# First norm of a two-layer diffusion step: order of the scale's loads, and unsplit weights for the first shift

## Chip, cores and metric

The kernel runs on one core of a Trainium2 chip. The metric is device time in microseconds, the median of several runs of one program. TensorE (PE) multiplies, VectorE (DVE), ScalarE (ACT) and GpSimd (POOL) do the elementwise work, and SyncE (SP) issues nearly all transfers, in order.

## The reference, cut to what matters

The model is one inference step of two hybrid layers over 128 context tokens and 512 latent tokens, 1024 wide. Each layer begins so:

```python
mod = silu(cond) @ w_ada[l] + b_ada[l]          # cond: c_ctx for context tokens, c for latent tokens
shift1, scale1, gate1, shift2, scale2, gate2 = split(mod, 6)
h = rmsnorm(x, norm1_g) * (1.0 + scale1) + shift1
xbc, dv, ... = split(h @ w_in, ...)             # one input projection
```

The rest (latent attention, differential attention, a scan, the output projection, a squared-ReLU network) is the same before and after the change. All of it is in float32.

## The kernel before

**Layout.** Features lie on the 128 partitions and the 640 tokens on the free axis, so x is eight tiles (k = 0 to 7) of 128 x 640, called `x`. Weights come in halves of 128 x 512: `wr` is a raw half, `wh` its rounded high part and `wl` the remainder. A product of float32 accuracy is made of three fast matmuls, `wh`*`zh`, `wh`*`zl` and `wl`*`zh`, where `zh` and `zl` are the same two parts of the scaled input. PE runs each of them in two column halves of 320, so one k of one unit takes six matmuls, and one k of two units twelve (`fm`, L312, matmul at L318).

**Scale and shift of the first norm.** `AdaPE` (L355) computes one 1024-wide slice of `mod` for both conditions: `first` is the scale (slice 1), `second` the shift (slice 0). The slice comes in two halves of 512 columns, and a half needs eight pieces `war` of 128 x 512 (256 KB), one per k. A step splits a piece into `wah` (ACT, L377) and `wal` (DVE or POOL, L378) and multiplies both by the small `sch` and `scz` (PE, L379 and L380, tile `adap`, four output rows, 512 columns). After eight steps `half` (L385) copies the result (`adarow`, ACT), turns it by four transposes (`adat`, PE), copies and sums (`adah`), and `ada_finish` (L335) adds the bias (`mod`); for the scale it also makes `amul`, for the shift the parts `shh` and `shl`.

**First products.** x is scaled by `amul` before its mean square is known (`scaled`, L488: `zh` on ACT, `zl` on DVE), and squares (`nsq`) are summed beside it. `first_units` (L546) multiplies `xbc0` and `xbc1` by it. Then `rows` (tile `nss`) and `spread` (tile `nrb`) make the row factors `nR`, and `out` applies them to the product (`un`, DVE). The shift enters the first two units as a product of raw weights and shift (`bshp`, L677), added later. For `xbc2` and `xbc3` the shift is put into the input itself (`normed`, L637: `nt` on DVE, `hhi` on ACT, `hlo` on DVE), so these products need the shift of their own k: k = 0 to 3 its first half, k = 4 to 7 its second. After them come the units `dv` (tile `tm`, L758 to L760).

**What sets the order.** Each engine works through its own queue in order. A scheduler orders the queues by its own estimate of times; `after` asks it to place instructions behind a given one. `LATE` gives how many steps of the shift follow each k of the first products (0, 0, 0, 0, 2, 4, 5, 5), and the rest follow them. `AP1` and `AP0` list the steps whose `wal` POOL makes. SP's queue holds, in this order: the first eight pieces of the scale, the four halves of `xbc0` and `xbc1`, four x tiles, `rows`, eight pieces of the scale, four x tiles, masks, seven raw halves, 16 pieces of the shift. Of the seven raw halves, two are of `xbc2` and five are asked for under the name `xbc3`, of which two are used; the other three are fetched and read by nothing.

Of the kernel before, what the change touches and what calls it, by code (L numbers as in the profile page):

```python
# [21 lines left out]
P = 128  # L22
D = 1024
KD = D // P
# [38 lines left out]
UNIT = {}  # L63
# [41 lines left out]
def build(nc, tc, a, ctx):  # L105
# [63 lines left out]
    def f(ap):  # L169
        return ap.bitcast(F32)  # L170
# [141 lines left out]
    def fm(outs, hi, lo, xh, xl, ks, first, last):  # L312

        for i, k in enumerate(ks):
            wh, wl = hi[:, i * P:(i + 1) * P], lo[:, i * P:(i + 1) * P]
            for w, xx, s, e in ((wh, xh, k == first, False), (wh, xl, False, False), (wl, xh, False, k == last)):
                for o, ts in outs:
                    pe.matmul(o, w, xx[k][:, ts], start=s, stop=e)  # L318

    def fm_unit(hi, lo, xh, xl, cut=None):  # L320
        ps = PA("fm")
# [10 lines left out]
    shh = [cp.tile([P, 2, KD, 2], F32R, name=f"shh{l}") for l in range(DEPTH)]  # L332
    shl = [cp.tile([P, 2, KD, 2], F32R, name=f"shl{l}") for l in range(DEPTH)]

    def ada_finish(l, j, ps, ms=slice(0, KD)):  # L335
# [8 lines left out]
        if j in (0, 3):  # L344
            evac_split(shh[l][:, j // 3, ms], shl[l][:, j // 3, ms], mods[l][:, j, ms])


# [5 lines left out]
    vec.tensor_tensor(out=sch[:, :, 2:4], in0=sc, in1=f(sch[:, :, 0:2]), op=ALU.subtract)  # L353

    class AdaPE:  # L355


        def __init__(self, l, j, on_pool):
# [9 lines left out]
        def step(self, n=1):  # L368
            for _ in range(n):
                if self.n == 2 * KD:  # L370
                    return
                h, k = divmod(self.n, KD)
                if k == 0:
                    self.ps = PB("adap")
                raw = self.raws[self.n]
                hi, lo = Y([P, 512], F32R, name="wah"), Y([P, 512], F32R, name="wal")
                act.copy(out=hi, in_=raw)  # L377
                (pool if self.n in self.on_pool else vec).tensor_tensor(out=lo, in0=raw, in1=f(hi), op=ALU.subtract)  # L378
                pe.matmul(self.ps[:4], sch[:, k, :], hi, start=(k == 0), stop=False)  # L379
                pe.matmul(self.ps[:4], scz[:, k, :], lo, start=False, stop=(k == KD - 1))  # L380
                self.n += 1
                if k == KD - 1:
                    self.half(h)

        def half(self, h):  # L385
            pt = PB("adat")
            row = X([4, 512], name="adarow")
            act.copy(out=row, in_=self.ps[:4])
            for m in range(4):
                pe.transpose(pt[:, 4 * m:4 * m + 4], row[:, m * P:(m + 1) * P], ident[:4, :4])  # L390
            p4 = pt[:, :16].rearrange("p (m q v) -> p m q v", q=2, v=2)
# [150 lines left out]
    def zhalves(ps, c=0):  # L542

        return [(ps[:, 0, c:HT + 2], slice(c, HT + 2)), (ps[:, 1, :HT], slice(HT + 2, T + 2))]

    def first_units(W, names, nrm, then=None, late=None):  # L546

        ps = [PA("fm") for _ in names]
        for k in range(KD):
            with after(nrm.last):  # L550
                if k == 4:
                    nrm.rows()
                if k == 5:
                    nrm.spread()
            if k == 6 and then:
                then()
            for n, p_ in zip(names, ps):
                hi, lo = W(n)
                fm(zhalves(p_, 0 if nrm.early else 2), hi[:, k * P:], lo[:, k * P:], nrm.zh, nrm.zl, [k], 0, KD - 1)
            if late:  # L560
                with after(nrm.mid):
                    late.step(LATE[k])
        return ps

# [6 lines left out]
    def mixing(l, nrm, fill, late=None, raws={}):  # L571
# [82 lines left out]
        W.ahead = AHEAD  # L654
        if late:
            with after(nrm.last):
                late.step(16)
                W.half(4)
            for k in range(3):
                normed(k)  # L660
        else:
            xps = [padded(None, z) for z in zs]
        ps = [PA("fm") for _ in range(2)]
        for k in range(KD):
            mark(f"{l}norm1")
            if k >= 3:
                normed(k)
            mark(f"{l}xbc")
            for j in range(2):
                hi, lo = W(f"xbc{2 + j}")  # L670
                fm(halves(ps[j]), hi[:, k * P:], lo[:, k * P:], hh, hl, [k], 0, KD - 1)
        if late:
            pb_ = PB("bshp")
            for j in range(2):
# [1018 lines left out]
    N_TAIL = 30  # L1693
    AHEAD = 1
    FETCHED, AHEADS = 7, 2
    AP1, AP0 = (1, 4), ()
    FILL = (2, 20, 9), (8, .01, 9)
    ROWS_POOL = ()
    CONV_POOL = ()
    ON_POOL = {f"xbc{j}" for j in range(2, 6)} | {"dv0", "dv1"}  # L1700
    LATE = (0, 0, 0, 0, 2, 4, 5, 5)
    N_STACK = 52
    N_SSD = 34
    N_PROJ = 28
# [260 lines left out]
    for h in range(2):  # L1965
        first.fetch()
        for n_ in ("xbc0", "xbc1") if h == 0 else ():
            for i in range(2):
                raws0[n_].append(G([P, 512], name="wr0"))
                o = UNIT[n_][0] + i * 512  # L1970
                nc.sync.dma_start(raws0[n_][i], a["W"][0, :, o:o + 512])
        for k in range(4 * h, 4 * h + 4):
            load_x(a["xT"], k)
        if h == 0:
            rows0 = load_rows(0)
# [4 lines left out]
    raws0.update({"xbc2": [raw_weights(0, "xbc2", h) for h in range(2)], "xbc3": [raw_weights(0, "xbc3", h) for h in range(NWR - 2)]})  # L1980
    second.fetch()
    second.fetch()
    nrm = Norm(False)
    act.copy(out=identr, in_=id_)
    first.step(8)
    for k in range(4):
        nrm.scaled(0, 0, k)
        if k == 1:
            last = nrm.last
    with after(last):  # L1990
        for k in range(4):
            first.step(2)
            nrm.square(k, vec)
    for k in range(4, 8):
        nrm.scaled(0, 0, k)
        nrm.square(k, vec)
        if k == 4:
            nrm.mid = nrm.last
# [131 lines left out]
```

## Time and profile before

| | us |
|---|---|
| median of 3 runs | 1838.31 (1832.51 to 1839.88) |
| the profiled execution | 1843.01 |
| its span | 1841.2 |
| PE busy | 1752.6 (95%) |
| DVE busy | 1330.3 (72%) |
| ACT busy | 828.8 (45%) |
| POOL busy | 464.5 (25%) |

The span runs from the first to the last instruction of the profiled execution; 1.8 us of its time lie outside. A row of a timeline is one or more like instructions in a row on one engine: start, duration, engine, line, what is written and read, and how many. What stands in brackets is the engine's idle time ahead of it and what ended that. Matmuls are pipelined: the distance between starts is what one costs, and its duration is longer. Matmuls in full float32 are recorded twice. PEclk is the granted clock of TensorE as a share of 2.4 GHz: 1.00 is 2.4 GHz and 0.50 is 1.2 GHz.

### The profile page before, as it was taken

The page shows a single profiled execution, that of the slowest core. Times are in us where ns is not written, and L with a number is a line of the kernel's source. Part 1 is how long each engine was busy: PE and PEld are TensorE (multiplying, and loading weights), DVE is VectorE, ACT ScalarE, POOL GpSimd, SP SyncE. Part 2 cuts the span into 40 slices and gives each one's busy share as a digit, 9 for nine tenths or more (in the row PEclk, how much of TensorE's full clock was granted, in tenths as well). Part 3 has the DMA queues.
Part 4 walks back from the last instruction along what each step waited for, and adds up shares of the span by engine and source line. Part 5 has one row for each costly group of instructions (what it writes and reads, how often), then busy time and mean ns, then how long its engine had stood idle before and what let it go on. Part 6 is the DMA issues. An engine that isn't in the chain of part 4 may idle for free. (4 is left out here: it accounts for less than half of the span.)

```text
span 1841.2 us, 31851 instructions
## 1 busy us (share of the span) xinstructions
PE 1752.6 (95%) x11764; PEld 1659.3 (90%) x11764; DVE 1330.3 (72%) x2788; ACT 828.8 (45%) x1737; POOL 464.5 (25%) x538
## 2 busy tenths in 40 slices
PE   6999999999989999999997999889999999999999
PEld 4798778998989999999997987779999999999998
DVE  6774867568578988685776778989677877475562
ACT  7553327554445452432544443387534445243340
POOL 1433433101120231404135244431003032130400
PEclk8899866899999999999999999889999999999999
DMA  9122113344143437264441232202424242525341
GB/s 336 56 78 71 52 35 88 103 136 146 32 136 117 138 100 260 93 213 154 149 159 48 76 107 68 69 25 84 138 88 127 86 131 81 186 87 161 112 157 56
DMA packets 122732, 209.02 MB, mean 114 GB/s; under 512 B 13392, under 2 KB 32720, under 8 KB 122576
## 3 DMA queue, kind: packets, MB, share of 16 engines
q1 hardware_dynamic: 122016, 206.80, 35.2%
q8 instruction: 93, 1.52, 0.3%
q14 instruction: 63, 0.52, 0.1%
q10 hardware_dynamic: 560, 0.18, 0.0%
HBM read 179.51 MB, written 27.43 MB: 112 GB/s over the span
## 5 line engine op out<-in xcount | busy, mean ns | idle before, releaser
L1775 ACT CAST wh<-wr 128x512 fp32r<-128x512 f32 x232 | 143.9, 621 | 316.0 <-PE fm L1805 205.2
L1805 PE MATMUL fm<-ul,wh 128*128 128x320 f32 x1024 | 235.0, 311 | 10.2 <-DVE ul L307 10.2
L1776 DVE TENSOR_TENSOR wl<-wr,wh 128x512 fp32r<-128x512 f32 x232 | 179.0, 780 | 79.8 <-issue 44.6
L1805 PE MATMUL fm<-uh,wh 128*128 128x320 f32 x1024 | 234.8, 310 | 0.1
L1805 PE MATMUL fm<-uh,wl 128*128 128x320 f32 x1024 | 234.5, 310 | 0.0
L1762 POOL TENSOR_TENSOR wS<-wr,wr 128x512 f32<-128x512 f32 x48 | 78.7, 1639 | 495.2 <-DMA wr<-in_W 213.9
L1805 PEld LDWEIGHTS fm<-ul,wh 128*128 128x128 f32 x1024 | 172.3, 189 | 11.3 <-DVE ul L307 11.3
L427 DVE SCALAR_TENSOR_TENSOR junk<-wa,crow 128x512 f32<-128x512 f32 x256 | 176.7, 739 | 7.4 <-DMA wa<-in_w_adaT 5.7
L1805 PEld LDWEIGHTS fm<-uh,wh 128*128 128x128 f32 x1024 | 172.4, 189 | 0.5 <-issue 0.3
L1805 PEld LDWEIGHTS fm<-uh,wl 128*128 128x128 f32 x1024 | 172.3, 189 | 0.0
L539 DVE SCALAR_TENSOR_TENSOR x<-fm,mod,x 128x128 f32<-128x128 f32 (+2 forms) x192 | 72.5, 432 | 107.7 <-PE fm L1805 104.7
L759 PE MATMUL tm<-wl,hhi 128*128 128x256 f32 (+2 forms) x400 | 120.0, 300 | 5.7 <-POOL wl L297 4.0
L1775 ACT CAST wh<-wS 128x512 fp32r<-128x512 f32 x96 | 59.8, 622 | 141.7 <-PE fm L1805 70.5
L758 PE MATMUL tm<-wh,hhi 128*128 128x256 f32 (+2 forms) x400 | 120.0, 300 | 3.0 <-DVE zth L779 2.4
L760 PE MATMUL tm<-wh,hlo 128*128 128x256 f32 (+2 forms) x400 | 119.2, 298 | 0.0
L296 ACT CAST wh<-wr 128x512 fp32r<-128x512 f32 (+2 forms) x108 | 66.8, 625 | 75.6 <-PE fm L318 34.6
L1805 PE MATMUL ffx<-eh,wh 128*128 128x320 f32 x288 | 89.4, 311 | 0.0
L1805 PE MATMUL ffx<-eh,wl 128*128 128x320 f32 x288 | 88.9, 309 | 0.0
L1805 PE MATMUL ffx<-el,wh 128*128 128x320 f32 x288 | 88.9, 309 | 0.0
L759 PEld LDWEIGHTS tm<-wl,hhi 128*128 128x128 f32 x400 | 80.2, 200 | 8.0 <-POOL wl L297 4.2
L539 DVE SCALAR_TENSOR_TENSOR x<-wo,mod,x 128x128 f32<-128x128 f32 (+1 forms) x144 | 57.0, 432 | 39.0 <-PE wo L318 38.5
L758 PEld LDWEIGHTS tm<-wh,hhi 128*128 128x128 f32 x400 | 80.1, 200 | 5.1 <-DVE zth L779 2.8
(386 smaller groups left out, 4837.1 us busy)
## 6 DMA issues: line engine op xcount, KB each, us to landing
wr<-in_W SPq DMA_DIRECT2D x351, 256.0 KB, 2.8
wa<-in_w_adaT SPq DMA_DIRECT2D x128, 256.0 KB, 4.5
xsave<-x SPq DMA_DIRECT2D x72, 320.0 KB, 2.2
x<-xsave SPq DMA_DIRECT2D x72, 320.0 KB, 4.0
war<-in_w_ada SPq DMA_DIRECT2D x32, 256.0 KB, 5.3
wa<-in_w_ada SPq DMA_DIRECT2D x32, 256.0 KB, 3.4
x<-in_xT SPq DMA_DIRECT2D x16, 320.0 KB, 5.5
out_yT<-x SPq DMA_DIRECT2D x8, 320.0 KB, 2.2
```

The costliest lines, as they stand in the source:

```text
L296: act.copy(out=hi[:, :w], in_=raw[:, :w])
L427: vec.scalar_tensor_tensor(out=junk, in0=raws[i], scalar=1.0, in1=row[v][h], op0=ALU.mult, op1=ALU.mult, accum_out=sum_)
L539: vec.scalar_tensor_tensor(out=x[m][:, t0:t0 + n], in0=src, scalar=mods[l][:, j, m, v:v + 1], in1=x[m][:, t0:t0 + n], op0=ALU.mult, op1=AL ...
L758: pe.matmul(ps[:, i, :n], hh[k][:, ts], hi[:, c:c + n], start=s, stop=False)
L759: pe.matmul(ps[:, i, :n], hh[k][:, ts], lo[:, c:c + n], start=False, stop=False)
L760: pe.matmul(ps[:, i, :n], hl[k][:, ts], hi[:, c:c + n], start=False, stop=e)
L1762: pool.tensor_tensor(out=box[key], in0=box[x0], in1=box[x1], op=op)
L1775: act.copy(out=hi, in_=raw)
L1776: vec.tensor_tensor(out=lo, in0=raw, in1=f(hi), op=ALU.subtract)
L1805: mm = pe.matmul(o, w_, x_[:, ts], start=s_, stop=e_, skip_group_check=on)
```

## The change

All 16 pieces of the scale are loaded first; then `rows`, x tiles 0 and 1, the first halves of `xbc0` and `xbc1`, x tiles 2 and 3, their second halves, x tiles 4 to 7, eight pieces of the shift, four raw halves (`xbc2` and `xbc3`), eight pieces of the shift, and the masks. The scale's 16 steps are written ahead of all scaling of x. For the shift `on_pool` is `None`: a step is one matmul of the raw piece by the unsplit `sc` (two output rows, 512 columns, full float32), with no cast and no subtraction, and `half` has no sum of parts; `shh` and `shl`, which the first norm doesn't read, are not made. `LATE` places eight steps behind k = 5, 6 and 7 of the first products (2, 3, 3), and two behind each of k = 0 to 3 of `xbc2` and `xbc3`. The row sums and factors come at k = 6 and 7 instead of 4 and 5. The three unread halves are no longer fetched.

```diff
@@ AdaPE.step
-                hi, lo = Y([P, 512], F32R, name="wah"), Y([P, 512], F32R, name="wal")
-                act.copy(out=hi, in_=raw)
-                (pool if self.n in self.on_pool else vec).tensor_tensor(out=lo, in0=raw, in1=f(hi), op=ALU.subtract)
-                pe.matmul(self.ps[:4], sch[:, k, :], hi, start=(k == 0), stop=False)
-                pe.matmul(self.ps[:4], scz[:, k, :], lo, start=False, stop=(k == KD - 1))
+                if self.on_pool is None:
+                    pe.matmul(self.ps[:2], sc[:, k], raw, start=(k == 0), stop=(k == KD - 1))
+                else:
+                    ...
@@ AdaPE.half
+            if self.on_pool is None:
+                act.copy(out=row[:2], in_=self.ps[:2])
+                for m in range(4):
+                    pe.transpose(pt[:, 2 * m:2 * m + 2], row[:2, m * P:(m + 1) * P], ident[:2, :2])
+                ada_finish(self.l, self.j, pt[:, :8].rearrange("p (m v) -> p m v", v=2), slice(4 * h, 4 * h + 4), False)
+                return
@@ first_units
-                if k == 4:
+                if k == (6 if late else 4):
                     nrm.rows()
-                if k == 5:
+                if k == (7 if late else 5):
                     nrm.spread()
...
             if late:
-                with after(nrm.mid):
+                with after([mm]):
                     late.step(LATE[k])
@@ mixing
             with after(nrm.last):
-                late.step(16)
                 W.half(4)
...
+            if late and k < 4:
+                with after([mm]):
+                    late.step(2)
@@ build
-    AP1, AP0 = (1, 4), ()
+    AP1, AP0 = (1, 4, 9, 12), None
-    LATE = (0, 0, 0, 0, 2, 4, 5, 5)
+    LATE = (0, 0, 0, 0, 0, 2, 3, 3)
...
+    first.fetch()
+    first.fetch()
+    rows0 = load_rows(0)
+    for i in range(2):
+        for k in range(2 * i, 2 * i + 2):
+            load_x(a["xT"], k)
+        for n_ in ("xbc0", "xbc1"):
+            ...
+    for k in range(4, KD):
+        load_x(a["xT"], k)
+    second.fetch()
+    raws0.update({n_: [raw_weights(0, n_, h) for h in range(2)] for n_ in ("xbc2", "xbc3")})
+    second.fetch()
...
-    first.step(8)
+    first.step(16)
+    for k in range(KD):
         nrm.scaled(0, 0, k)
         nrm.square(k, vec)
```

Where instructions went, in the engines' queues:

ACT before, from the last cast of the scale's first half to the first scaling of x (`wr_10` to `wr_13` are the halves of `xbc0` and `xbc1`):

```order
L377 CAST wah_254<-war_116 128x512
L296 CAST wh_412<-wr_10_118 128x512
L296 CAST wh_422<-wr_11_120 128x512
L296 CAST wh_426<-wr_12_122 128x512
L296 CAST wh_488<-wr_13_124 128x512
L388 COPY adarow_261<-adap_211 4x512
L981 ACTIVATE ea_1339<-rows_134 128x16
L393 COPY adah_267<-adat_260 128x8
L493 ACTIVATE zh_272<-x_126,amul_88 128x128
```

ACT after, at the same place (`wr_21`, `wr_25` are the halves of `xbc0`, `wr_22`, `wr_26` those of `xbc1`):

```order
L382 CAST wah_303<-war_130 128x512
L994 ACTIVATE ea_1243<-rows_134 128x16
L296 CAST wh_406<-wr_21_140 128x512
L296 CAST wh_416<-wr_25_148 128x512
L296 CAST wh_420<-wr_22_142 128x512
L296 CAST wh_472<-wr_26_150 128x512
L399 COPY adarow_255<-adap_205 4x512
L404 COPY adah_261<-adat_254 128x8
L382 CAST wah_309<-war_132 128x512
L504 ACTIVATE zh_327<-x_136,amul_88 128x128
```

Fifteen of the scale's 16 casts now stand ahead of the copy `adarow` of its first half, and so does, as before, the split of all four halves.

PE before, from the end of the scale's first half to the first product (`fm`):

```order
L379 MATMUL adap_211<-wah_254,sch 4x512
L380 MATMUL adap_211<-wal_255,scz 4x512
L390 MATMUL adat_260<-identr,adarow_261 128x4 x4
L318 MATMUL fm_410<-zh_272,wh_412 128x320 x2
L318 MATMUL fm_411<-zh_272,wh_426 128x320 x2
```

PE after, at the same place:

```order
L384 MATMUL adap_205<-wah_248,sch 4x512
L385 MATMUL adap_205<-wal_249,scz 4x512
L401 MATMUL adat_254<-identr,adarow_255 128x4 x4
L384 MATMUL adap_266<-wah_267,sch 4x512
L385 MATMUL adap_266<-wal_268,scz 4x512
L384 MATMUL adap_266<-wah_273,sch 4x512
```

The 16 matmuls of the scale's second half now stand between the transposes of the first half and the first product; before, they stood among the products.

PE before, in the products of `xbc2` and `xbc3`, from k = 3 to k = 4 (`hhi_754` is k = 3, `hhi_775` is k = 4):

```order
L318 MATMUL fm_708<-hhi_754,wh_715 128x320 x2
L318 MATMUL fm_708<-hlo_755,wh_715 128x320 x2
L318 MATMUL fm_708<-hhi_754,wl_716 128x320 x2
L318 MATMUL fm_707<-hhi_775,wh_676 128x320 x2
L318 MATMUL fm_707<-hlo_776,wh_676 128x320 x2
```

PE after, at the same place (`hhi_648` is k = 3, `hhi_679` is k = 4, `adap` here is the shift's second half):

```order
L318 MATMUL fm_595<-hhi_648,wl_603 128x320 x2
L379 MATMUL adap_616<-war_196,sc 2x512
L379 MATMUL adap_616<-war_198,sc 2x512
L396 MATMUL adat_670<-identr,adarow_671 128x2 x4
L690 MATMUL bshp_768<-mod_86,wr_21_140 128x2 x4
L690 MATMUL bshp_768<-mod_86,wr_25_148 128x2 x4
L690 MATMUL bshp_768<-mod_86,wr_22_142 128x2 x4
L690 MATMUL bshp_768<-mod_86,wr_26_150 128x2 x4
L318 MATMUL fm_594<-hhi_679,wh_563 128x320 x2
```

Two steps of the shift stand behind each of k = 0 to 3, and the shift's last transposes and the whole of `bshp` stand ahead of k = 4; before, both came elsewhere, the transposes ahead of k = 0 and three quarters of `bshp` behind k = 7.

## Rows read from the trace of the kernel before

**Rows 1.** The page, busy us (share of the span) and count of one engine.
```profile
PE 1752.6 (95%) x11764; PEld 1659.3 (90%) x11764; DVE 1330.3 (72%) x2788; ACT 828.8 (45%) x1737; POOL 464.5 (25%) x538
```

**Rows 2.** Stretches: start:end, length, then as the heading says.
```profile
core 0: us, PE busy (x) PEld busy (x) DVE busy (x) ACT busy (x) POOL busy (x), PEclk, DMA share, GB/s
...
53.80:64.70 10.90, 6.84 (x31) 3.70 (x29) 10.64 (x24) 5.31 (x14) 2.60 (x2) 0.76 0.16 48
...
83.10:200.00 116.90, 116.79 (x789) 104.43 (x789) 76.52 (x151) 50.53 (x118) 42.79 (x50) 0.94 0.26 76
200.00:260.00 60.00, 57.43 (x314) 46.22 (x313) 42.65 (x84) 15.01 (x37) 18.92 (x15) 0.84 0.09 27
```

**Rows 3.** ACT's timeline, 10 to 17 us: start, us, instruction, idle ahead of it.
```profile
10.22 0.62 ACT L377 CAST wah<-war 128x512 fp32r<-128x512 f32 x1 [0.16 <-DMA war<-in_w_ada]
...
16.61 0.21 ACT L981 ACTIVATE ea<-rows 128x16 f32<-128x16 f32 x1 [2.77 <-DMA rows<-in_rows]
```

**Rows 4.** PE's, ACT's and DVE's timelines, 18 to 40 us, one after another.
```profile
18.58 1.43 PE L318 MATMUL fm<-zh,wh 128*128 128x320 f32 x4 [4.28 <-ACT zh L493]
...
31.80 0.41 PE L390 MATMUL adat<-identr,adarow 4*128 4x4 f32 x4 [0.66 <-ACT adarow L388]
...
39.17 1.41 PE L318 MATMUL fm<-zh,wh 128*128 128x320 f32 x4
...
31.18 0.57 ACT L388 COPY adarow<-adap 4x512 f32<-4x512 f32 x1 [3.89 <-PE adap L380]
31.66 1.98 ACT L482 ACTIVATE nsq<-x 128x640 f32<-128x640 f32 x3
...
36.08 1.01 ACT L493 ACTIVATE zh<-x,amul 128x128 fp32r<-128x128 f32 x2 [1.12 <-DVE amul L342]
...
38.40 1.01 DVE L494 SCALAR_TENSOR_TENSOR zl<-x,amul,zh 128x128 fp32r<-128x128 f32 x2
```

**Rows 5.** PE's timeline: split matmuls of 512 columns, then full float32 ones.
```profile
29.59 0.39 PE L379 MATMUL adap<-wah,sch 128*4 128x512 f32 x1
29.82 0.40 PE L380 MATMUL adap<-wal,scz 128*4 128x512 f32 x1
...
1194.26 2.05 PE L1303 MATMUL kva<-wukv,ckc 128*128 128x512 f32 x2 [0.92 <-DMA wukv<-in_W]
...
1227.14 1.02 PE L1303 MATMUL kva<-wukv,cqf 128*128 128x512 f32 x2
1228.00 0.60 PE L1391 MATMUL pT<-identr,prob 128*128 128x128 f32 x4
```

**Rows 6.** DVE's timeline, then PE's, 53 to 84 us.
```profile
53.83 1.54 DVE L526 TENSOR_TENSOR un<-fm,nR 128x640 f32<-128x640 f32 x2
...
58.05 4.71 DVE L643 SCALAR_TENSOR_TENSOR nt<-x,amul,nR 128x128 f32<-128x128 f32 x10
...
63.94 3.52 DVE L647 SCALAR_TENSOR_TENSOR hlo<-nt,mod,hhi 128x512 fp32r<-128x512 f32 x7
...
64.73 0.90 PE L318 MATMUL fm<-hlo,wh 128*128 128x320 f32 x2 [2.81 <-DVE hlo L647]
...
80.23 0.46 PE L318 MATMUL fm<-hhi,wl 128*128 128x320 f32 x2
80.53 2.73 PE L677 MATMUL bshp<-mod,wr 128*128 128x2 f32 x24
83.12 0.41 PE L758 MATMUL tm<-wh,hhi 128*128 128x272 f32 x1
```

**Rows 7.** Stretches by the level of TensorE's clock (PEclk), columns as in rows 2.
```profile
18.60:21.80 3.20, 3.20 (x12) 3.20 (x13) 2.80 (x5) 3.20 (x7) 0.00 (x0) 0.50 1.05 397
...
35.80:42.20 6.40, 5.16 (x21) 4.95 (x22) 6.37 (x14) 6.12 (x14) 0.00 (x0) 0.50 1.05 384
42.40:59.30 16.90, 15.57 (x90) 10.30 (x90) 14.47 (x27) 12.49 (x29) 10.11 (x6) 1.00 0.29 85
59.50:69.60 10.10, 7.29 (x28) 6.89 (x28) 10.10 (x25) 5.22 (x13) 0.34 (x6) 0.50 0.01 2
...
83.30:86.60 3.30, 3.30 (x16) 3.30 (x16) 3.30 (x4) 0.50 (x2) 0.84 (x4) 0.50 0.62 177
```

More of the change, by code (lines that the diff above doesn't have):

```diff
@@ L317, in fm @@
                 for o, ts in outs:
-                    pe.matmul(o, w, xx[k][:, ts], start=s, stop=e)
+                    mm = pe.matmul(o, w, xx[k][:, ts], start=s, stop=e)
+        return mm
     def fm_unit(hi, lo, xh, xl, cut=None):
@@ L333, in build, with ada_finish @@
     shl = [cp.tile([P, 2, KD, 2], F32R, name=f"shl{l}") for l in range(DEPTH)]
-    def ada_finish(l, j, ps, ms=slice(0, KD)):
+    def ada_finish(l, j, ps, ms=slice(0, KD), parts=True):
         n = ms.stop - ms.start
@@ L343, in ada_finish @@
                                      in1=g.unsqueeze(2).to_broadcast([P, n, 2]), op0=ALU.add, op1=ALU.mult)
-        if j in (0, 3):
+        if j in (0, 3) and parts:
             evac_split(shh[l][:, j // 3, ms], shl[l][:, j // 3, ms], mods[l][:, j, ms])
@@ L375, in step @@
                 raw = self.raws[self.n]
-                hi, lo = Y([P, 512], F32R, name="wah"), Y([P, 512], F32R, name="wal")
-                act.copy(out=hi, in_=raw)
-                (pool if self.n in self.on_pool else vec).tensor_tensor(out=lo, in0=raw, in1=f(hi), op=ALU.subtract)
-                pe.matmul(self.ps[:4], sch[:, k, :], hi, start=(k == 0), stop=False)
-                pe.matmul(self.ps[:4], scz[:, k, :], lo, start=False, stop=(k == KD - 1))
+                if self.on_pool is None:
+                    pe.matmul(self.ps[:2], sc[:, k], raw, start=(k == 0), stop=(k == KD - 1))
+                else:
+                    hi, lo = Y([P, 512], F32R, name="wah"), Y([P, 512], F32R, name="wal")
+                    act.copy(out=hi, in_=raw)
+                    (pool if self.n in self.on_pool else vec).tensor_tensor(out=lo, in0=raw, in1=f(hi), op=ALU.subtract)
+                    pe.matmul(self.ps[:4], sch[:, k, :], hi, start=(k == 0), stop=False)
+                    pe.matmul(self.ps[:4], scz[:, k, :], lo, start=False, stop=(k == KD - 1))
                 self.n += 1
@@ L558, in first_units @@
                 hi, lo = W(n)
-                fm(zhalves(p_, 0 if nrm.early else 2), hi[:, k * P:], lo[:, k * P:], nrm.zh, nrm.zl, [k], 0, KD - 1)
+                mm = fm(zhalves(p_, 0 if nrm.early else 2), hi[:, k * P:], lo[:, k * P:], nrm.zh, nrm.zl, [k], 0, KD - 1)
             if late:
-                with after(nrm.mid):
+                with after([mm]):
                     late.step(LATE[k])
@@ L670, in mixing @@
                 hi, lo = W(f"xbc{2 + j}")
-                fm(halves(ps[j]), hi[:, k * P:], lo[:, k * P:], hh, hl, [k], 0, KD - 1)
+                mm = fm(halves(ps[j]), hi[:, k * P:], lo[:, k * P:], hh, hl, [k], 0, KD - 1)
+            if late and k < 4:
+                with after([mm]):
+                    late.step(2)
         if late:
@@ L1964, in build @@
     raws0 = {"xbc0": [], "xbc1": []}
[L1965 to L1972, printed above, removed]
-            load_x(a["xT"], k)
-        if h == 0:
-            rows0 = load_rows(0)
+    first.fetch()
[3 more added lines that the diff above has]
+        for k in range(2 * i, 2 * i + 2):
+            load_x(a["xT"], k)
+        for n_ in ("xbc0", "xbc1"):
+            raws0[n_].append(G([P, 512], name="wr0"))
+            o = UNIT[n_][0] + i * 512
+            nc.sync.dma_start(raws0[n_][i], a["W"][0, :, o:o + 512])
+    for k in range(4, KD):
[3 more added lines that the diff above has]
+    second.fetch()
     mk = X([P, 4, P], name="masks")
@@ L1979, in build @@
     nc.sync.dma_start(kinds, a["kinds"])
-    raws0.update({"xbc2": [raw_weights(0, "xbc2", h) for h in range(2)], "xbc3": [raw_weights(0, "xbc3", h) for h in range(NWR - 2)]})
-    second.fetch()
-    second.fetch()
     nrm = Norm(False)
     act.copy(out=identr, in_=id_)
-    first.step(8)
[L1986 to L1994, printed above, removed]
+    first.step(16)
+    for k in range(KD):
         nrm.scaled(0, 0, k)
         nrm.square(k, vec)
-        if k == 4:
-            nrm.mid = nrm.last
     with after(nrm.last):
```

## Prediction

> **What bounds the kernel now.** I read the page first: TensorE is busy for 95% of the span [rows 1], no other engine for more than 72%. A change to the first 90 us therefore counts only through the moment at which TensorE reaches its unbroken work. The table of stretches shows that moment [rows 2]: from 83.1 us to 200 us TensorE is busy for 116.79 of 116.9 us. It begins with the first matmul of the `dv` unit, at 83.12 us [rows 6]. So I ask one thing: when does that matmul start after the change? A delay there is passed on in full as far as 200 us. Ahead of it TensorE is not full: from 53.8 to 64.7 us it is busy for 6.84 of 10.9 us [rows 2], it waits 4.28 us ahead of its first product, and nothing but ten small matmuls stands between the transposes at 31.80 and the product at 39.17 [rows 4]. These holes are what the change could fill.
>
> **First product: later.** Before, the first product starts at 18.58 us [rows 4], right after half of the scale. Now it needs more. In ScalarE's new order the copy `adarow` of the first half stands behind the splits of all four halves of `xbc0` and `xbc1`, and the last of these halves is now loaded behind all 16 scale pieces, `rows` and four tiles of x. The rate: before, four weight halves (256 KB each), four x tiles (320 KB) and `rows` (212 KB), 2.58 MB, lie between the landing of the eighth scale piece (10.22 us) and that of `rows` (16.61 us) [rows 3], so 403 GB/s. After, eight pieces, `rows`, four tiles and four halves, 4.67 MB, follow the eighth piece: 11.6 us, so 21.8 us. The split takes 0.62 us [rows 3], `adarow` to transposes 0.62 us, the transposes 0.41 us [rows 4]: they end at 23.45 us.
>
> Here the Trainium skill speaks against the loads: "DMA: Bandwidth & Descriptors", Specifications, gives an HBM limit of about 358 GB/s for a core. By it, as an estimate, the 4.67 MB take 13.1 us, the chain behind them comes 1.5 us later, and the +5.0 us of the sum below would be +6.5; the rows' 403 GB/s decide.
>
> Next come the 16 matmuls of the scale's second half. Their weights are there early, but in TensorE's new order they stand behind those transposes. A matmul of this form takes 0.23 us at full clock [rows 5], twice that at half. TensorE will have idled for several us, and behind such idleness products ran at half clock for 3 to 5 us (18.58 to 21.8 us; 64.73 to 69.6) [rows 4, 6, 7]. I take 4 us from 23.1: 27.1 us with eight matmuls done, then eight at 0.23: first product at **29.0 us**, bounds 27.1 (all at full clock) and 30.8 (all at half).
>
> **Back level at k = 4.** Two matmuls of a product take 0.30 us (80.23 to 80.53) [rows 6], so one k of two units, twelve matmuls, 1.8 us. k = 0 to 3 (7.2) and the transposes (0.41) end at 36.6 us. ScalarE scales the first tile some 2 us behind the transposes' start (a copy, three small sums and one subtraction that stands among them), 25.2 us, and four tiles at 1.01 us [rows 4] by 29.3, copies `adarow` to 30.0, takes eight squares at 0.66 [rows 4] and a copy to 35.4; the second half's `amul` follows VectorE's sums as before, so the fifth tile is scaled at about 36.1, as now (36.08) [rows 4]. Its product starts one tile later, near 37.1, instead of 39.17 [rows 4]. The lost 10 us of the start are thus already paid back: the earlier scale of before only led into the hole from 31 to 37 us.
>
> **Streams instead of splits.** Per step the change removes a ScalarE cast (0.62 us [rows 3]), a VectorE subtraction of about the same length and two split matmuls of 0.23 us, and adds one unsplit matmul of 512 columns. The nearest row for it is `kva`: two records, 0.86 us from start to start at full clock (1227.14 to 1228.00); at half clock the two records last 2.05 instead of 1.02 us [rows 5], twice as long. So TensorE pays 0.86 - 0.46 = 0.40 us more for each of 16 steps, 6.4 us in all, at full clock.
>
> k = 4 to 7 are paced by VectorE's `zl` (1.01 us a tile [rows 4]) at first, then by TensorE: with `zl` of the fifth tile near 38.8 and of the sixth near 39.8, k = 5 ends at 41.8 us; then six streams (5.2), `nss` (1.1, ten records at the 0.108 us of `bshp`), k = 6 and 7 (3.6) and ten small matmuls of `nrb` (1.2): 52.9 us, and with the copy of the factors `un` starts at 53.4. Before it started at 53.83 [rows 6]. TensorE's streams cover here what the splits cost before; if they ran at half clock, 3 us more.
>
> **VectorE's gain.** Before, `nt` starts at 58.05, 2.7 us after `un` has ended [rows 6]: subtractions of the shift's pieces stand between. Now `un` (1.54) leads straight to eight `nt` (0.47 each, 3.8) and the shift's sum: 58.9. The first `hhi` takes 1.0 us more, and the order now puts the first `hlo` ahead of the last four pairs of `nt`, so the first product of `xbc2` starts at 59.9, with `hlo` at about 61. Before, TensorE waited for `hlo` until 64.73 [rows 6]. Gain here: 3 to 4 us. It is the only place where the removed work was on the path.
>
> **The second half of the shift.** Eight streams stand between k = 0 to 3 of `xbc2` and `xbc3`. VectorE delivers one `hlo` tile in 1.0 us (seven in 3.52) [rows 6], TensorE needs 1.8 us for its products: it never waits there, so nothing hides the streams. From 59.9: four k (7.2), eight streams (6.9), half clock for 4 us after the idle stretch (2.0): 76.0 us. Only then can `adarow`, transposes and sum of the second half run, 1.5 us (0.62 and 0.41 of rows 4 and two small operations), and TensorE has nothing else queued. `bshp`, 32 records, now comes before k = 4: 24 took 2.59 us [rows 6], so 3.45; then four k, 7.2. The `dv` matmul starts at 76.0 + 1.5 + 3.45 + 7.2 = **88.15 us** against 83.12: **+5.0 us**. `bshp` is followed by a half-clock spell before (83.3 to 86.6 us) [rows 7]; I leave the same spell, 1.6 us, in both.
>
> Three weight halves that nothing reads are no longer loaded (0.79 MB, 2 us of transfer). That transfer ends near 42 us beside other work: nothing. The later changes of order (a few rows each in the scan) I cost at nothing, between -3 and +3, the 2.6 us that TensorE idles from 200 to 260 being what could be won or lost of that kind [rows 2].
>
> **The sum.** Profiled execution: 1843.0 us, span 1841.2, the other 1.8 us unchanged; +5.0 gives 1848.0. This execution lies 4.7 us above the median of the runs, 1838.3, so the forecast for the median is 1838.3 + 5.0 = **1843 us**.
>
> **Rivals.**
> A, as above, +2 to +8 us: 0.50.
> B, the delay is not felt, 0.24. Either the clock stays full from 59.9 us and behind `bshp` (2.0 + 1.6 us back: +1.4), or the stage after 200 us, where TensorE idles 2.6 us [rows 2], absorbs part of it. About 1839.5. For it: 16 streams keep TensorE fed; against: TensorE idles some 5 us before 59.9, longer than the 2.81 us before 64.73 [rows 6].
> C, slower, 0.20. The half-clock spells of before last 6.4 and 10.1 us [rows 7], the second with products in it. If the clock stays low through the streams between k = 0 and 3, the 14.1 us of work from 59.9 us cost up to 14.1 more instead of 2.0, +17.1 in all, 1855; one spell like that of 59.5 to 69.6, plus one like that of 35.8 to 42.2, gives 5.0 + 3.0 + 3.2 = +11.2, 1849.5 (half of 10.1, less the 2.0 already counted, and half of 6.4). Slower by over 0.5% (9.2 us, about what a measurement of this kernel can tell) begins where half-clock stretches beyond A's reach 8.4 us, 4.2 us lost. Against: with split matmuls in the streams' place the clock was full from 42.4 to 59.3 us [rows 7].
> The Trainium skill, "TensorE: Matmul & The Clock Gate", Why this matters for your kernels, asks for dense matmuls without idle gaps; by that rule the new idle stretches, 55 to 60 and about 76, count against the change, and interleaved streams for it. The spell at 59.5 us behind idle work agrees [rows 7].
> D, faster by over 0.5%, 0.06. If all 16 streams fell into TensorE's idle time, 13.8 us would vanish from A, and with the spell behind `bshp` gone 1.6 more: 5.0 - 15.4 = -10.4, 1828. Against: TensorE takes its queue in order, and each stream stands between two products whose operands are ready.
>
> **How the numbers follow.** A's time is the forecast. Range 1834 to 1851: below, B's +1.4 with the spread of the runs shown (-5.8 to +1.6 us round the median); above, C's +11.2 with 1.6. That leaves out the upper part of C and D, about 0.2. Slower by over 0.5%: C, 0.20; faster: D, 0.06; within: A and B, 0.74.
>
> **What would show it.** First product near 29 us behind sixteen `adap` matmuls; a fifth tile scaled at 36; `un` near 53; first `hlo` product near 61; eight streams of 0.86 us, then a hole, `bshp` and k = 4; `dv` near 88. Wrong: a `dv` start below 84 or above 92; streams at 0.43 us or far above 0.9; a clock at half between 64 and 76 us; or a stretch after 200 us that differs by more than 3 us.

## Result: slower by 0.58%, about twice the forecast

| | before | after |
|---|---|---|
| median, us | 1844.87 (17 runs, 1832.51 to 1851.98) | 1850.74 (17 runs, 1842.33 to 1865.48) |
| ratio, 95% interval | | 1.0058 (1.0039 to 1.0076) |
| the profiled execution, its span | 1843.01, 1841.2 | 1850.74, 1849.0 |
| first dv matmul | 83.12 | 92.77 |

The ratio compares runs taken side by side and is about +10.7 us (7.2 to 14.0). The forecast was +5.0 us, within 0.5% of before. The base was off too: over 17 runs the kernel before has a median of 1844.87 us, and the three runs that I had seen gave 1838.31. So only the difference is judged here.

The page of after, busy time of each engine:

```profile
PE 1752.7 (95%) x11764; PEld 1648.0 (89%) x11764; DVE 1317.2 (71%) x2766; ACT 821.5 (44%) x1717; POOL 464.1 (25%) x540
```

VectorE and ScalarE are relieved of 13 and 7 us against [rows 1]; TensorE is busy for as long as before. What counts is again the way to `dv`. PE's timeline of after (start, us, instruction, idle ahead of it and what ended that), to be read against [rows 4 to 6]:

```profile
23.51 0.58 PE L401 MATMUL adat<-identr,adarow 4*128 4x4 f32 x4 [10.46 <-ACT adarow L399]
24.02 0.59 PE L384 MATMUL adap<-wah,sch 128*4 128x512 f32 x1
28.67 0.59 PE L385 MATMUL adap<-wal,scz 128*4 128x512 f32 x1
30.03 0.76 PE L318 MATMUL fm<-zh,wh 128*128 128x320 f32 x4
38.15 0.86 PE L318 MATMUL fm<-zh,wh 128*128 128x320 f32 x4 [0.30 <-ACT zh L504]
47.70 2.74 PE L379 MATMUL adap<-war,sc 128*2 128x512 f32 x6
50.37 0.56 PE L318 MATMUL fm<-zh,wh 128*128 128x320 f32 x2
53.28 1.38 PE L529 MATMUL nrb<-identr,r 128*128 128x128 f32 x10
57.19 0.41 PE L396 MATMUL adat<-identr,adarow 2*128 2x2 f32 x4 [0.72 <-ACT adarow L394]
61.69 1.44 PE L318 MATMUL fm<-hhi,wh 128*128 128x320 f32 x4 [4.09 <-ACT hhi L657]
62.92 0.74 PE L318 MATMUL fm<-hlo,wh 128*128 128x320 f32 x2
77.21 1.88 PE L379 MATMUL adap<-war,sc 128*2 128x512 f32 x4
79.75 0.41 PE L396 MATMUL adat<-identr,adarow 2*128 2x2 f32 x4 [0.67 <-ACT adarow L394]
80.09 3.73 PE L690 MATMUL bshp<-mod,wr 128*128 128x2 f32 x32
83.68 1.41 PE L318 MATMUL fm<-hhi,wh 128*128 128x320 f32 x4
92.77 0.39 PE L771 MATMUL tm<-wh,hhi 128*128 128x272 f32 x1 [0.26 <-ACT xpad L613]
```

ACT's and DVE's timelines of after, the lines that judge the split ahead of `adarow` and the start of `un`:

```profile
21.32 1.66 ACT L296 CAST wh<-wr 128x512 fp32r<-128x512 f32 x3 [2.40 <-DMA wr<-in_W]
22.88 0.57 ACT L399 COPY adarow<-adap 4x512 f32<-4x512 f32 x1
55.26 1.55 DVE L537 TENSOR_TENSOR un<-fm,nR 128x640 f32<-128x640 f32 x2 [9.18 <-ACT nR L530]
```

Stretches of after (start:end, length, busy time of PE, PEld, DVE, ACT, POOL, then PEclk, DMA share, GB/s):

```profile
10.20:21.30 11.10, 2.84 (x9) 0.59 (x7) 7.49 (x8) 5.79 (x11) 5.31 (x8) 0.74 1.04 393
23.10:29.10 6.00, 5.59 (x17) 1.96 (x17) 5.19 (x13) 4.55 (x11) 0.00 (x0) 0.50 1.05 392
61.69:66.63 4.94, 4.94 (x14) 3.38 (x15) 4.94 (x11) 2.67 (x6) 0.00 (x0) 0.50 0.00 0
67.70:79.60 11.90, 11.39 (x49) 6.07 (x48) 1.20 (x3) 1.77 (x3) 2.75 (x5) 1.00 0.05 12
83.70:87.00 3.30, 3.30 (x14) 3.30 (x14) 1.54 (x3) 0.47 (x2) 2.86 (x6) 0.50 0.09 25
```

The reader is to see three half-clock spells, each behind a wait or behind `bshp`, and the holes that remain: 10.46 us ahead of the first transposes and 4.09 us ahead of `xbc2`.

One caution on `dv` as the mark. The spell behind `bshp` lies behind the `dv` start in the kernel before (83.3 to 86.6 us, [rows 7]) and ahead of it in after (83.7 to 87.0). The first transposes of `xs` (tile `xT`), some 30 us later, lie past it in both: 113.90 us before, 122.05 after. So the delay that TensorE carries is **8.15 us**, not 9.65. Beside each run below stand both marks, the length from `dv` to the first feed-forward product (`fm` from `uh`), and from there to the last matmul's start.

| kernel | dv | xT | dv to ff | ff to end | against before, us (95%) |
|---|---|---|---|---|---|
| before | 83.12 | 113.90 | 498.0 | 1255.3 | 0 |
| before_again | 83.35 | 114.13 | 495.2 | 1258.2 | |
| after | 92.77 | 122.05 | 488.1 | 1263.2 | +10.7 (7.2 to 14.0) |
| after_again | 91.71 | 120.97 | 488.0 | 1260.2 | +10.7 (6.6 to 14.6) |
| delay2 | 87.57 | 116.86 | 490.1 | 1266.5 | +7.2 (4.1 to 10.5) |
| delay6 | 91.42 | 120.69 | 490.6 | 1263.0 | +10.0 (5.3 to 14.6) |
| delay11 | 91.67 | 120.96 | 501.1 | 1265.9 | +14.9 (9.0 to 20.8) |
| after_split | 88.31 | 117.60 | 506.0 | 1259.9 | +16.8 (11.8 to 21.8) |
| after_loads_before | 91.59 | 120.82 | 492.1 | 1261.9 | +11.8 (7.2 to 16.2) |
| before_streams | 88.00 | 117.28 | 492.9 | 1265.7 | +4.2 (-1.3 to 9.8) |
| after_early_second | 89.11 | 118.37 | 493.1 | 1262.7 | +7.9 (3.1 to 12.5) |
| after_early_rows | 87.36 | 116.64 | 492.4 | 1269.9 | +6.8 (2.6 to 11.1) |
| after_warm | 92.74 | 122.01 | 495.5 | 1260.3 | +10.5 (5.5 to 15.3) |
| before_mended | 82.49 | 111.75 | 494.8 | 1262.9 | +3.7 (-0.2 to 7.7) |
| after_split_early | 79.73 | 109.00 | 493.9 | 1266.3 | +0.7 (-4.4 to 5.9) |
| before_no_dead_loads | 83.54 | 112.81 | 484.4 | 1257.9 | -1.8 (-5.9 to 2.2) |

The last column is the ratio of side-by-side runs less one, times 1844 us; the others are one execution each.

### The profile page after: what moved, and what is told of

Its sections match the earlier page's. It is cut to its first block, busy times and chain, and to the rows that moved or that the text cites. A ratio compares the mean times of both kernels' runs of the same rounds, so it can differ in the third digit from the quotient of the medians.

```text
span 1849.0 us, 31800 instructions
## 1 busy us (share of the span) xinstructions
PE 1752.7 (95%) x11764; PEld 1648.0 (89%) x11764; DVE 1317.2 (71%) x2766; ACT 821.5 (44%) x1717; POOL 464.1 (25%) x540
## 5 line engine op out<-in xcount | busy, mean ns | idle before, releaser
L1818 PE MATMUL fm<-ul,wh 128*128 128x320 f32 x1024 | 235.0, 311 | 10.2 <-DVE ul L307 10.2
L1775 POOL TENSOR_TENSOR wS<-wr,wr 128x512 f32<-128x512 f32 x48 | 81.2, 1692 | 492.1 <-DMA wr<-in_W 297.5
L772 PEld LDWEIGHTS tm<-wl,hhi 128*128 128x128 f32 x400 | 79.7, 199 | 8.8 <-POOL wl L297 4.7
```

The costliest lines, as they stand in the source:

```text
L772: pe.matmul(ps[:, i, :n], hh[k][:, ts], lo[:, c:c + n], start=False, stop=False)
L1775: pool.tensor_tensor(out=box[key], in0=box[x0], in1=box[x1], op=op)
L1818: mm = pe.matmul(o, w_, x_[:, ts], start=s_, stop=e_, skip_group_check=on)
```

## Experiments

**Is a delay ahead of dv passed on?** Idle work between `bshp` and `dv`, nothing else edited (11, 6 or 2 matmuls). The order behind it was meant to stay, but the scheduler changed it: by the traces, TensorE keeps the order of before only as far as 184.75 us of that kernel, and of the 11440 matmuls from `dv` on 188 (delay2, delay6) and 282 (delay11) stand at other places; in after it is 263.

```diff
+            for i in range(11):
+                pe.matmul(pb_[:2, 8:512], sc[:, i % KD], raws["xbc0"][0][:, 8:512], start=True, stop=True)
```

> The kernel before with one addition: eleven unsplit float32 matmuls of 504 columns, whose result nothing reads, stand on TensorE between the last bshp matmul and the first dv matmul (tile tm). Everything behind them keeps its order. At 0.85 us each the first dv matmul should start near 92.4 us instead of 83.12, about as late as in the changed kernel (92.77). Theory 1 (what is lost ahead of dv is passed on to the end): time 9 to 10 us above the kernel before, ratio 1.005. Theory 2 (the waits of the scan, 190 to 270 us, swallow it, and what the changed kernel lost came about behind them): 0 to +3 us, ratio 1.000 to 1.0015, and in the trace the offset against the kernel before falls below 3 us by 300 us.

> The same with six such matmuls. dv at 88.2 us, the moment that the prediction gave for the changed kernel. Passed on one to one: +5.1 us, ratio 1.0028. If any shift loses 5 us more: ratio 1.0055.

> The kernel before with two unsplit matmuls of 504 columns, whose result nothing reads, between bshp and dv; all else in its order. dv at 84.9 us. Passed on one to one: +1.7 us, ratio 1.0009. If the kernel before stands at a moment that any shift loses (half-clock spells behind dv): +5 us or more, ratio 1.003 or higher.

PE's timeline of delay11, then of delay2, and the stretches of delay2 and delay6:

```profile
82.29 9.46 PE L679 MATMUL bshp<-wr,sc 128*2 128x504 f32 x22
91.67 0.39 PE L760 MATMUL tm<-wh,hhi 128*128 128x272 f32 x1
```
```profile
84.33 3.31 PE L679 MATMUL bshp<-wr,sc 128*2 128x504 f32 x4
87.57 0.39 PE L760 MATMUL tm<-wh,hhi 128*128 128x272 f32 x1
```
```profile
84.30:87.60 3.30, 3.30 (x6) 0.39 (x6) 3.30 (x4) 0.40 (x1) 1.07 (x4) 0.55 0.71 199
84.60:91.40 6.80, 6.80 (x13) 1.09 (x12) 6.80 (x8) 0.86 (x2) 1.09 (x4) 0.75 0.35 104
```

Theory 2 falls: nothing swallows the delay. With `xT` 2.96, 6.79 and 7.06 us later the time rises by 7.2, 10.0 and 14.9 us. So these delays cost at least their length; each run is 3 to 8 us above that, and the intervals of delay2 (4.1 to 10.5) and delay11 (9.0 to 20.8) leave their 2.96 and 7.06 us out. How much of that excess belongs to the delay, and how much to the other order behind 185 us, these runs do not separate. The two matmuls of delay2 fell into the half-clock spell behind `bshp` and took 3.24 us instead of 1.7. The six of delay6 took 6.82 us instead of 5.1 (`dv` at 91.42, not 88.2), while the eleven of delay11 ran at 0.85 us each.

**Which part of the change delays dv?** Split pieces instead of streams, all else as in after:

```diff
-    AP1, AP0 = (1, 4, 9, 12), None
+    AP1, AP0 = (1, 4, 9, 12), ()
```

> The changed kernel with the shift's pieces split again (cast on ScalarE, subtraction on VectorE, two fast matmuls), the loads, the places of the steps and the late row sums left as they are. Theory A (the unsplit streams are the cost): a step takes 0.46 instead of 0.86 to 0.9 us of TensorE, so the first dv matmul comes 4 to 7 us earlier than 92.77, at 86 to 89 us, and the time falls by as much if the delay is passed on. Theory B (the order of loads and of the scale's steps is the cost): dv stays within 2 us of 92.77. Theory C (VectorE and ScalarE, relieved by the streams, set the pace ahead of the products of xbc2): un, nt and hlo come later again, dv at 93 us or later.

`dv` at 88.31 us: the streams are worth 4.5 us there (3.4 against after_again), as theory A had it. But the time did not fall with it; if anything it rose. That gain was lost behind `dv` (506.0 us to the feed-forward part). Two stretches of after_split, then one of after, show how:

```profile
88.31:594.30 505.99, 486.16 (x3199) 445.06 (x3199) 344.93 (x791) 236.48 (x541) 121.27 (x170) 0.89 0.30 89
178.90:213.10 34.20, 34.20 (x121) 27.11 (x120) 14.90 (x28) 11.19 (x27) 10.72 (x7) 0.50 0.15 41
92.77:580.86 488.09, 468.88 (x3199) 430.94 (x3200) 346.13 (x791) 235.77 (x541) 121.89 (x170) 0.92 0.30 93
```

The same matmuls keep TensorE busy for 17.3 us longer, at a mean granted clock of 0.89 instead of 0.92. One half-clock spell alone lasts from 178.9 to 213.1 us, with TensorE busy throughout. What set it off is not shown.

The loads and the scale's steps of the kernel before (its two subtractions on GpSimd too), streams and places of after:

```diff
+    for h in range(2):
+        first.fetch()
         ...
+    first.step(8)
+    for k in range(4):
+        nrm.scaled(0, 0, k)
         ...
```

> The changed kernel with the loads and the scale's steps in the order of the kernel before (half of the scale, then x, then the other half between the first products; without the three unread halves), the unsplit streams and their places kept. Theory B (load order is the cost): first product at 18.6 us again and dv 2 to 5 us earlier than 92.77. Theory A (streams are the cost): first product at 18.6 us, but the product of k = 4 waits for the scale's second half until 39 us as in the kernel before, so dv lies within 1.5 us of 92.77 (or later).

First product at 18.29 us, `dv` at 91.59: within 1.2 us of after. Theory A holds here: a first product nearly 12 us earlier is worth next to nothing.

Streams alone, in the kernel before (with the edits of `step` and `half` that the change has):

```diff
-    AP1, AP0 = (1, 4), ()
+    AP1, AP0 = (1, 4), None
```

> The kernel before with the shift's steps as unsplit streams, nothing else changed (load order, places and row sums as before). The second eight streams then fall into the stretch from 54 to 62 us in which TensorE waits for VectorE, and all of bshp ahead of the second product of xbc2. Theory A as a price per stream (16 times 0.40 us, wherever they stand): dv at 83.1 + 6.4 = 89.5 us. Theory A as a matter of place (a stream costs only where TensorE would else have a product ready): first eight cost up to 3 us, second eight nothing, VectorE is relieved by 16 subtractions, dv at 80 to 85 us, time within 0.25% of before or faster.

`dv` at 88.0 us, `xT` 3.4 us late. The "place" version was too hopeful. PE's timeline of before_streams:

```profile
65.10 1.05 PE L686 MATMUL bshp<-mod,wr 128*128 128x2 f32 x8
66.85 5.11 PE L686 MATMUL bshp<-mod,wr 128*128 128x2 f32 x24
71.83 0.88 PE L318 MATMUL fm<-hlo,wh 128*128 128x320 f32 x2
```

The second eight streams end later than VectorE's wait lasted, and the scheduler then puts all of `bshp` ahead of the first `hlo` product, which it delays by some 5 us at half clock.

All streams among the first products, none behind:

```diff
-    LATE = (0, 0, 0, 0, 0, 2, 3, 3)
+    LATE = (0, 0, 0, 0, 0, 4, 6, 6)
-            if late and k < 4:
-                with after([mm]):
-                    late.step(2)
```

> The changed kernel with all 16 streams of the shift among the first products (4, 6 and 6 behind k = 5, 6 and 7) and none between the products of xbc2 and xbc3; its shift is then whole before these products start, and bshp stands ahead of them. Theory P (place: eight streams, the turn of the second half and bshp between k = 3 and k = 4 are the cost): the eight streams (7 us) fill the 4 us in which TensorE waits ahead of 61.7 us, the turn (1 us) lies ahead of it too, so dv comes 3 to 5 us earlier than 92.77, at 88 to 90 us. Theory S (a stream costs its 0.4 us wherever it stands, and VectorE's chain un, nt, hlo starts where the row factors let it): TensorE reaches xbc2 some 4 us later than 61.7 and saves 8 us behind it, but bshp (3.5 us at full, 5 to 7 us at half clock) stays ahead of hlo, so dv moves by less than 2 us.

`dv` at 89.11 us, 3.7 us earlier than after (2.6 than after_again), in theory P's range; but the first `hlo` product came only at 72.99 us, since `bshp` stood ahead of it at half clock, as theory S feared:

```profile
67.84 5.28 PE L687 MATMUL bshp<-mod,wr 128*128 128x2 f32 x24 [2.29 <-DVE mod L340]
72.99 0.88 PE L318 MATMUL fm<-hlo,wh 128*128 128x320 f32 x2
```

Row sums and factors behind k = 3 and 4 again:

```diff
-                if k == (6 if late else 4):
+                if k == 4:
                     nrm.rows()
-                if k == (7 if late else 5):
+                if k == 5:
                     nrm.spread()
```

> The changed kernel with the row sums and factors behind k = 3 and 4 again (as in the kernel before) instead of behind k = 5 and 6. Theory R (the late row factors hold VectorE's un back: it starts at 55.26 us, 0.8 us behind the copy of the factors): un starts when k = 7 is done, near 52 to 53 us, the first product of xbc2 1 to 2.5 us earlier than 61.69, and dv as much earlier, 90 to 92 us. Rival (TensorE, not the factors, sets that moment: the streams that stand ahead of the last products): dv within 0.7 us of 92.77.

The largest effect of any single part. PE's and DVE's timelines, and the stretch of the streams:

```profile
46.08 1.28 PE L529 MATMUL nrb<-identr,r 128*128 128x128 f32 x10
47.29 7.03 PE L379 MATMUL adap<-war,sc 128*2 128x512 f32 x16
56.75 0.85 PE L318 MATMUL fm<-hhi,wh 128*128 128x320 f32 x4 [1.30 <-ACT hhi L657]
87.36 0.39 PE L771 MATMUL tm<-wh,hhi 128*128 128x272 f32 x1 [0.24 <-ACT xpad L613]
```
```profile
47.96 1.55 DVE L537 TENSOR_TENSOR un<-fm,nR 128x640 f32<-128x640 f32 x2 [4.44 <-ACT nR L530]
55.48 0.17 DVE L340 TENSOR_TENSOR mod<-adat,vecs 128x8 f32<-128x8 f32 x1 [2.27 <-PE adat L396]
```
```profile
47.20:54.90 7.70, 7.12 (x18) 1.27 (x16) 5.25 (x10) 1.22 (x3) 1.84 (x2) 1.00 0.39 108
```

With the factors early, the scheduler puts all eight streams of the first half behind the last product. `un` starts at 47.96 instead of 55.26 us, the streams run while VectorE makes `un` and `nt`, and `xbc2` starts 4.94 us earlier. `dv` comes 5.4 us earlier than in after (4.35 than in after_again). The streams are not wholly free there either: VectorE then waits 2.27 us for the shift's first half. In after, the same streams ahead of the products of k = 6 and 7, with the late factors, hold up `un` and all behind it; which of the two counts for more, this run does not separate. Both theories had it too small.

**Does the half clock follow the wait?** Four idle matmuls in the 4.09 us ahead of `xbc2`:

```diff
+            warm = PB("warm")
+            with after([nrm.mm]):
+                for i in range(4):
+                    pe.matmul(warm[:2], sc[:, i], raws["xbc0"][0], start=True, stop=True)
```

> The changed kernel with four unsplit matmuls of 512 columns, whose result nothing reads, between the transposes of the shift's first half (57.19 us) and the first product of xbc2 (61.69 us), where TensorE waits 4.09 us. They take 3.5 us and end before the product's operand is there. Theory H (the half-clock spell from 61.69 to 67.7 us follows from that wait; it costs 3 us): the spell is gone or begins later, the streams between k = 0 and 1 take 1.88 instead of 2.58 us, and dv comes 2 to 3 us earlier than 92.77, or the spell only moves. Rival (the spell comes whatever TensorE does there): the products at 62 to 67.7 us run at half clock as before, dv within 0.7 us of 92.77 (91.7 in the second execution).

PE's timeline and stretches of after_warm:

```profile
56.35 3.60 PE L673 MATMUL warm<-wr,sc 128*2 128x512 f32 x8
60.52 0.85 PE L318 MATMUL fm<-hhi,wh 128*128 128x320 f32 x4 [0.57 <-ACT hhi L658]
76.87 5.89 PE L695 MATMUL bshp<-mod,wr 128*128 128x2 f32 x32
92.74 0.40 PE L776 MATMUL tm<-wh,hhi 128*128 128x272 f32 x1 [0.26 <-ACT xpad L614]
```
```profile
56.40:79.60 23.20, 21.97 (x95) 11.71 (x95) 12.48 (x29) 8.02 (x17) 2.91 (x8) 0.97 0.08 24
79.60:88.30 8.70, 8.70 (x36) 8.70 (x37) 2.43 (x5) 1.48 (x4) 6.25 (x21) 0.50 0.08 19
```

The spell of 61.69 to 66.6 us is gone, so it did follow from the wait: from the first `hhi` product to the second transposes 16.02 us instead of 18.06. Then `bshp` came, and in its midst began a spell of 8.7 us instead of 3.3: from `bshp` to `dv` 15.87 us instead of 12.68. The spell had only moved, and the time is that of after.

**Does the trace repeat, and is there a better kernel?** The two kernels themselves in other executions:

> The changed kernel itself in other executions. Up to dv the trace should repeat: first product 29 to 30.5, dv 91.5 to 93 us. In the first trace the stretch from dv to the first product of the feed-forward part (fm from uh) lasted 488 us against 498 before, and the loss came back as half clock in layer 1. Theory 1 (the order behind dv is worth nothing; which products of the scan fall into half clock differs from one execution to the next): this stretch lies anywhere from 488 to 506 us, and the ratio again at 1.004 to 1.008. Theory 2 (the order behind dv gains 10 us of its own): the stretch is 488 us again, within 2.

> The kernel before in another execution, for its trace alone. If what stands behind dv differs by half-clock spells from one execution to the next: the stretch from dv (83.1) to the first product of the feed-forward part is not 498 us again but 490 to 505. If it belongs to the order of the program: 498 within 2, and from there to the end 1255 within 2.

Up to `dv` both repeat within 1.1 us, and the ratio of after came out the same, 1.0058. Behind it after keeps its 488 us; before_again is 2.8 and 2.9 us off the first trace in the two stretches. The kernel before without the three unread halves (five halves of `xbc3` asked for become two) has another order behind `dv`: 360 of the 11440 matmuls stand elsewhere than in before, and 574 elsewhere than in after:

> The kernel before without the loads of the three unread halves, nothing else edited. Up to dv the order is the same, dv at 83 us; behind dv the planner places some of the scan's products and small matmuls otherwise, much as in the changed kernel. If only dv counts: ratio 1.000, within 0.001. If the order behind dv is worth something: below 0.998 (the changed kernel's stretch from dv to the feed-forward part is 488 us against 495 to 498) or above 1.002 (what follows is then lost in layer 1).

Its stretch is even shorter, 484.4 us, in an execution that was the fastest of its twelve (1832.6 us); over all its runs it is 0.9990 (0.9968 to 1.0012). So the unread loads cost nothing that can be measured, and neither a gain nor a loss from this order of the scan is shown.

Two attempts to mend. before_mended: in the kernel before, row sums one k later, four subtractions on GpSimd, `nt` of a later k behind `hlo`, no unread loads. after_split_early: the loads of after, split pieces, early rows, the same rule for `nt`, no steps between the products of `xbc2`:

```diff
@@ before_mended
+    AP1, AP0 = (1, 4), (9, 11, 13, 15)
+                if k == (5 if late else 4):
+                    nrm.rows()
+                if k == (6 if late else 5):
+                    nrm.spread()
@@ both
+                with after([lows[2 * k - 5]]) if late else contextlib.nullcontext():
+                    normed(k)
@@ after_split_early
+    AP1, AP0 = (1, 4, 9, 12), ()
+    LATE = (0, 0, 0, 0, 2, 4, 5, 5)
```

> The kernel before, with the split kept and three small edits: the row sums and factors one k later (behind k = 4 and 5), four of the shift's subtractions (pieces 9, 11, 13, 15) on GpSimd instead of VectorE, and the nt of each k from 3 on behind the hlo of the k three before; the three unread halves are not loaded. If TensorE's waits ahead of dv are what counts (theory 1): nss no longer stands ahead of k = 4 (2 us), VectorE reaches nt 2 to 3 us earlier, and the first hlo product comes at 60 to 62 instead of 64.73; dv at 77 to 80 us, time 3 to 6 us below the kernel before, ratio 0.997 to 0.998. If something behind dv sets the end: ratio 1.000.

> The changed kernel's loads and scale, with the rest put where TensorE waits or other engines are idle: the shift's pieces split (all steps among or behind the first products, as in the kernel before), the row sums behind k = 3 and 4, and the nt of each k from 3 on behind the hlo of the k three before. If the places of the streams, the late rows and the turn between k = 3 and 4 are the whole cost of the change, nothing of it is left, and what its loads gain (k = 4 at 38 instead of 39.2 us, no wait of TensorE from 31 to 37 us) shows: dv at 77 to 82 us, time 0 to 6 us below the kernel before. If the loads themselves cost (first product at 30 us): dv at 83 us or later.

`xT` came 2.15 and 4.90 us earlier than before, but the times are +3.7 and +0.7 us, neither told apart from no change. The loads of after, freed of the rest, thus cost nothing ahead of `dv`: there this version is the best of all. No kernel is shown to beat the one before.

## Why the prediction was wrong, step by step

**What held.** The moment of `dv` as the thing to ask for, its sign, and the delay "passed on in full as far as 200 us": 8.15 us at `xT`, and 9.7, so 1.5 more, at 175 us (`cqss`, 184.79 against 175.09). The paid-back start held as well: k = 4 was 1.05 us late against the forecast and 1.02 us early against before. Unread loads at nothing: -1.8 us, not told from zero. On the DMA rate the rows' 403 GB/s stood nearer than the Trainium skill's 358 ("DMA: Bandwidth & Descriptors", Specifications): the stretch 10.2 to 21.3 us moved 393 GB/s.

**What failed is sizes on the path.** By the forecast's own moments, with what each step added to the miss:

| moment | forecast | after | added |
|---|---|---|---|
| first scale matmul behind the transposes | 23.45 | 24.02 | +0.6 |
| first product | 29.0 | 30.03 | +0.5 |
| product of k = 4 | 37.1 | 38.15 | 0.0 |
| un | 53.4 | 55.26 | +0.8 |
| first xbc2 product | 59.9 | 61.69 | -0.1 |
| streams of k = 3 over (adarow of ScalarE at 79.12) | 76.0 | 79.1 | +1.3 |
| bshp | 77.5 | 80.09 | -0.5 |
| k = 4 of xbc2 | 80.95 | 83.68 | +0.1 |
| dv | 88.15 | 92.77 | +1.9 |

- *One split, 0.62 us, between the last half's landing and `adarow`*: three casts stood there, 1.66 us. In ScalarE's order the first half of `xbc1`, loaded earlier, stands behind the second of `xbc0`.
- *"I take 4 us" at half clock, twice*: the spells lasted to 29.1 us (12 of the scale's 16 matmuls, not 8) and from 61.69 to 66.6 us (4.9 us at half clock, so 2.5 us lost, not 2).
- *0.86 us a stream*: three take 2.67 us (47.70 to 50.37), 0.89 each; over 16 streams 0.5 us.
- *"The same spell in both" behind `bshp`*: it was there, 83.7 to 87.0 us, but ahead of `dv`. This 1.6 us is no loss against before and drops out at `xT`. Without it the miss is 3.1 us: 8.15 against 5.0.

**The step that was wrong in kind** is "TensorE's streams cover here what the splits cost before", and with it "the only place where the removed work was on the path". I compared `un` with the kernel before (53.4 against 53.83) and saw no loss. But before, the removed work held `un` up as well. VectorE's subtractions stood ahead of it, and the products themselves ended only at 52.98 us, because 16 split matmuls of the shift stood among those of k = 4 to 7 (DVE's and PE's timelines of before):

```profile
47.37 6.54 DVE L378 TENSOR_TENSOR wal<-war,wah 128x512 fp32r<-128x512 f32 x9
52.52 0.46 PE L318 MATMUL fm<-zh,wl 128*128 128x320 f32 x2
```

The change took both away: after_early_rows shows `un` at 47.96. In after, the streams ahead of k = 6 and 7, with the late factors, used up that gain: 7.3 us at `un`, 4.9 at the first `xbc2` product, 5.4 at `dv`. The streams' arithmetic counts too (4.5 us at `dv`, after_split), but the forecast had a price for it, 0.40 us a stream. The two effects overlap, since together they exceed the 8.15 us.

**The rivals.** B ("not felt"): no. D: no. C had the size (+11.2) but another mechanism: the clock stayed full through the streams from 67.7 to 79.6 us. By the Trainium skill, "TensorE: Matmul & The Clock Gate", Why this matters for your kernels, idle gaps between matmuls cost clock; after_warm agrees for the spell at 61.69 us, and shows that filling one gap need not win anything. A had the mechanism, but its range of +2 to +8 did not hold 10.7. Of the signs of being wrong, a `dv` above 92 was met by 0.8 us, a half clock behind 64 us as far as 66.6, and stretches behind 200 us that differ by more than 3 us by 10 and 8.

**What stays open.** The later parts were costed at 0 (±3), and the traces differ there by more. The parts from `dv` to the feed-forward part and from there to the last matmul's start, two rows of before and the second of after (its first stands at after_split):

```profile
83.12:581.11 497.99, 479.84 (x3200) 439.55 (x3200) 344.44 (x791) 233.13 (x537) 122.45 (x169) 0.89 0.30 91
581.11:1836.50 1255.39, 1210.55 (x8243) 1171.60 (x8242) 927.86 (x1884) 541.63 (x1087) 315.37 (x317) 0.98 0.36 116
580.86:1844.20 1263.34, 1214.26 (x8243) 1173.14 (x8242) 923.78 (x1884) 541.78 (x1087) 315.56 (x317) 0.97 0.36 116
```

In the first part after is 10 us shorter, and that is clock: 0.92 against 0.89, and TensorE busy for 11.0 us less with the same matmuls; the second executions of both kernels repeat it. In the second part after is 8 us longer, of which 4.2 us are waits of TensorE (49.1 against 44.8 us idle; 48.1 against 45.0 in the second executions). There before, before_again and before_no_dead_loads have 1255 to 1258 us, the other thirteen traces 1260 to 1270, with an earlier `dv` (79.7 us) and a later one alike, and with the same matmuls partly in another order. The delay runs and the two mended kernels lost 3 to 8 us there or near, so an earlier `xT` was not passed on either. Whether a shift as such costs this, or the order, the runs don't tell. Of the measured 10.7 us, 7.1 to 8.2 us are shown ahead of `xT`, and the rest is within the interval. The forecast missed by 5.7 us: 3.1 are the steps above, and the cause of the other 2.6, behind `xT`, stays open.

## To carry to other kernels

Work put into an in-order queue is free only where that engine would have waited: ask of each piece which instruction stands behind it, and compare with what that instruction could do after the change, not with when it ran before. When a change removes a wait, look first for what now ends the stretch. And take a difference of half a per cent from side-by-side runs: three runs of one kernel put the base 6.6 us off here.

## What was not expected of the hardware

- A stretch in which TensorE is busy throughout can be followed by half clock, and need not be. `bshp`, 32 records of two-column matmuls, ended in 3.3 us at 0.50 in after, and in after_warm a spell of 8.7 us began in its midst. In the kernel before its last 24 records ended in such a spell too ([rows 7], 83.3 us), but not in before_no_dead_loads, with the same 24 records ahead of `dv` at 83.54 us:

```profile
83.50:86.90 3.40, 3.40 (x29) 3.40 (x29) 3.40 (x3) 0.73 (x2) 1.64 (x5) 1.00 0.68 179
```

- Half clock can last while TensorE is busy: 34.2 us in after_split (178.9 to 213.1 us).
- Keeping TensorE busy ahead of `xbc2` with four idle matmuls took one spell away and lengthened the next; `dv` did not move (92.77 and 92.74 us).
